# Earlier decode-state loads, an order for the down projection, and two wider spacings in a hybrid decoder step

## The chip, the cores and the metric

The kernel runs on one core of a Trainium2 chip. A core has TensorE (PE, matrix multiplication into the PSUM banks; its weight loads are listed apart as PEld), VectorE (DVE), ScalarE (ACT), GpSimd (POOL) and SyncE (SP), which here issues all DMAs from one queue. Each engine takes its instructions in a fixed order, and waits on semaphores for the others. The metric is the time of one execution in device microseconds; lower is better. The median of three runs is compared.

## What is computed

One inference step of a one-layer decoder, in float32, for a prompt of 1024 tokens and for 8 decode sequences of 4 tokens (32 tokens). D_MODEL is 1024, D_FF is 2816.

```python
def half_ffn(x, j, gpre, gpost):
    y = swiglu(rmsnorm(x, g[gpre]), ffn_w_gate[l, j], ffn_w_up[l, j], ffn_w_down[l, j])
    return x + 0.5 * rmsnorm(y, g[gpost])

x = half_ffn(x, 0, 0, 1)
h = rmsnorm(x, g[2])
(qm, km, vm, om, ip, fp), (qa, ka, va) = split_proj(h, w_in[l], b_gate[l])
u_m, new_m = mlstm_heads(qm, km, vm, om, ip, fp, mstate, mlstm_norm_gain[l], h.dtype)
...
x = x + rmsnorm(u @ w_out[l], g[3])
x = half_ffn(x, 1, 4, 5)
```

Here swiglu is `(silu(x @ w_gate) * (x @ w_up)) @ w_down`. The mLSTM has 4 heads, each with a 128 × 128 state matrix C and a normaliser n. The prompt starts from a zero state. Each of the 8 decode sequences brings its own C and n, from which its output is computed (`q @ C`) and which is then updated (decay × C + k v) and returned.

## The kernel before

**Tiles.** The 1056 tokens are four column blocks q = 0 to 3 of 264 columns (256 prompt tokens and 8 decode tokens). Two blocks form a half g. Activations lie transposed, features on the 128 partitions. Each float32 operand is split into a high part, which ScalarE casts (L200), and a low part, which VectorE subtracts (L201); a product is three matmuls: high × high, high × low, low × high. `K.od.now` is the planner's clock: a matmul of 264 columns adds 0.0025 + 264 / 2400 = 0.1125.

**Order.** `Order` is a planner in the kernel's own Python. The main line emits matmuls and advances the clock; side tasks (generators, `od.spawn`) are stepped when the clock reaches their due time, and a `yield w` sets the next due time w planner microseconds later. This gives the order of the program's text. The library then puts each engine's instructions in order when the program is built: the place in the text is the priority, but an instruction that is held back (by an operand, or by a buffer that isn't free) may be passed by later ones that are ready. After that the order in each engine's queue is fixed. `tc.issue_after(x)` keeps the instructions of its block behind x in the queue of x's engine, without a semaphore.

**Buffers.** A pool `slot` has 64 tiles of 128 × 528 floats (NSLOT). The sums of x, h, the reloaded h, the projections and the decode states all come from it. Weights come in through 3 `raw` tiles (L225). PSUM has banks `mm` (3), `a` (2), `b` (2) and `c` (1).

**Gate and up.** `ffn` runs 11 pairs p of hidden blocks; all but the first use a Strassen-like scheme of seven products (`PROD`) for each of gate (`mat` 0) and up (`mat` 1). Each product is 12 matmuls for each half g. Several of them add up in the `mm` and `b` banks in several steps, so partial sums must be copied out before the next product adds to the same bank: `nc.scalar.copy(sc[n][:, g], ps)` (L961) after the first, third and fifth product, and VectorE sums (L972, L978, L980) with them. The results h go to DRAM (`store_h`, L1027), except those of the last pair.

**Down.** `load_h` is a side task that brings h back for two blocks q at a time: per step m (of 22) two DMAs of 132 KB into slots `hq` (L1042) and a split on ScalarE and VectorE, then `yield HW` with HW = 0.6. It is first spawned at the beginning of the last pair's up half (L938); slots come free as the sums of x are used for the last time. Matmuls `pd` need h for each m. A later `load_h` (L995) prepares the next two blocks during the down projection.

**Decode.** `mlstm_sample` is the side task of the decode sequences. `state(b)` takes a slot, issues the DMA of C (L1635, 256 KB) and lets GpSimd put n beside it (L1636). Four states are loaded at its beginning, then two more at the beginning of each later pair of sequences, ahead of which the previous pair's updated states have been stored (L1696). In between it computes decayed scores `E`, masked keys (`kr`, its transposes `tT`, `kw`) and masked queries `qm`. Each pair then runs `sinter` (queries × C, output of 32 partitions), `sU` (keys × values, 32 rows) and the VectorE update L1691. The matmuls run between those of the output gates `po`, and later of the output projection `pw`.

**End.** For the last block q = 3, class `Last` brings output and residual back to token-major form. `residual` loads x, and after 14 planner microseconds does six groups of four transposes `xT` into a `b` bank, each copied out by ScalarE (L673), with `yield 2.0` after each group. `first`, `second` and `store_y` of block 2 use `b` banks as well (`yT`).

Of the kernel before, what the change touches and what calls it, by code (L numbers as in the profile page):

```python
# [1 line left out]

# [1 line left out]

# [27 lines left out]

XW = [2.0, 0.15, 0.2, 4.0, 3.0, 0.5]
PW = [4.0, 5.0, 1.0, 6.0, 4.5]
HW = 0.6

NHELD, NS = 5, 2
PQ = {1: [4.0, 8.0, 0, 8.0], 2: [2.0, 8.0, 0, 6.0], 3: [3.0, 7.0, 3.0, 0]}
# [113 lines left out]
def pe(K, out, lhsT, rhs, start=True, stop=True, tr=False, **kw):  # L152
    n = int(np.prod(rhs.shape[1:]))
    if tr:
        K.nc.tensor.transpose(out, lhsT, rhs)  # L155
        K.od.now += 0.11
        return
    K.nc.tensor.matmul(out, lhsT, rhs, start=start, stop=stop, **kw)  # L158
    if rhs.dtype == F32R:
        K.od.now += 0.0025 + (n if n >= 213 else 256) / 2400  # L160
    else:
        K.od.now += (4 if rhs.dtype == F32 else 1) * max(n, 64) / 2400


def nm(K, s):
# [479 lines left out]
class Last:  # L645
# [16 lines left out]
    def residual(self):  # L662
        K = self.K
        t = [slot(K, "x") for _ in range(4)]
        for kp in range(4):
            K.nc.sync.dma_start(t[kp], K.xs[self.q][kp])
        yield 14.0
        for x in range(2):
            for j in range(3):
                ps = bank(K, "xT", "b")  # L670
                self.turn(t, x, j, ps)
                self.x[j][x] = slot(K, "xT")[:, 0:512]
                K.nc.scalar.copy(self.x[j][x], ps)  # L673
                yield 2.0

    def block(self, mo, ps):
        K, nc = self.K, self.K.nc
# [216 lines left out]
def ffn(K, phase, j, gpost, nxt, gpre=None):  # L894
    nc, od = K.nc, K.od
    hs = {}
    for p in range(MT // 2):
        sg = {}
        if p == 0 and phase == 1:
            first_pair(K, sg)  # L900
            for (m, g), t in sg.items():
                hs[m, g] = store_h(K, m, g, t)
            continue
        if p < NPLAIN:

            ws = {}
            for q in range(NQ):
                g, s = q // 2, slice((q % 2) * QW, (q % 2) * QW + QW)
                for mat in range(2):
                    for m in range(2):  # L910
                        if q == 0:
                            ws[mat, m] = [od.take() for _ in range(2)]
                        if (m, g) not in sg:
                            sg[m, g] = slot(K, "h")
                        ps = bank(K, "pl", "ab"[mat])[:, 0:QW]
                        for k in range(KT):
                            od.need(("b", phase - 1, q, k // 2))
                            xh, xl = [x[:, k % 2] for x in K.X[q][k // 2]]
                            wh, wl = [w[:, k % 4] for w in ws[mat, m][k // 4]]
                            pe(K, ps, wh, xh, start=(k == 0), stop=False)  # L920
                            pe(K, ps, wh, xl, start=False, stop=False)
                            pe(K, ps, wl, xh, start=False, stop=(k == 7))
                            od.tick()
                        if p == 0 and (q, mat, m) in SUMS[phase]:
                            od.spawn(sums(K, phase - 1, SUMS[phase][q, mat, m]))
                        d = sg[m, g][:, s]
                        if mat == 0:
                            nc.scalar.activation(d, ps, AF.Silu)
                        else:
                            nc.vector.tensor_tensor(d, d, ps, op=ALU.mult)  # L930
            for (m, g), t in sg.items():
                hs[2 * p + m, g] = store_h(K, 2 * p + m, g, t)
            continue
        if phase == 1 and p == 4:
            mix_setup(K)
        for mat in range(2):
            if mat and p == MT // 2 - 1:
                od.spawn(load_h(K, hs, (0, 1)))  # L938
            bk, sc = {}, [None] * 3
            for i, (xi, tag, new) in enumerate(PROD):  # L940
                wh, wl = od.take()
                for g in range(NG):
                    if new:
                        bk[tag, g] = bank(K, "gu", tag)[:, 0:QW]
                    ps = bk[tag, g]
                    od.need(("S", phase - 1, g))
                    for k in range(4):
                        if xi > 2:
                            od.need(("s", phase - 1, g, xi, k // 2))
                        xh, xl = K.S[g][xi][k // 2]  # L950
                        xh, xl = xh[:, k % 2], xl[:, k % 2]
                        kw = {} if new else dict(skip_group_check=True)
                        pe(K, ps, wh[:, k], xh, start=(new and k == 0), stop=False, **kw)
                        pe(K, ps, wh[:, k], xl, start=False, stop=False, **kw)
                        pe(K, ps, wl[:, k], xh, start=False, stop=(k == 3), **kw)
                        od.tick()
                    if i in (0, 2, 4):
                        n = i // 2
                        if sc[n] is None:
                            sc[n] = pair(tmp(K, "sc", 2 * QW))  # L960
                        nc.scalar.copy(sc[n][:, g], ps)  # L961
                    for m, t, at, tg, n in OUT:
                        if at != i:
                            continue
                        if mat == 0:
                            if (m, g) not in sg:
                                sg[m, g] = slot(K, "h")
                            d = sg[m, g][:, t * QW:(t + 1) * QW]
                            if n is None:
                                nc.scalar.activation(d, bk[tg, g], AF.Silu)  # L970
                            else:
                                nc.vector.tensor_tensor(d, bk[tg, g], sc[n][:, g], op=ALU.add)  # L972
                                nc.scalar.activation(d, d, AF.Silu)  # L973
                        else:
                            d = sg[m, g][:, t * QW:(t + 1) * QW]
                            src = bk[tg, g]
                            if n is not None:
                                nc.vector.tensor_tensor(sc[n][:, g], src, sc[n][:, g], op=ALU.add)  # L978
                                src = sc[n][:, g]
                            nc.vector.tensor_tensor(d, d, src, op=ALU.mult)  # L980
        for (m, g), t in sg.items():
            if p < MT // 2 - 1:
                hs[2 * p + m, g] = store_h(K, 2 * p + m, g, t)
            else:
                hs[2 * p + m, g] = t
    h = K.h
    npd = 0
    steps = STEPS[phase]
    for si, step in enumerate(steps):
# [2 lines left out]
        last = Last(K, step[0], gpost) if nxt is None and si + 1 == len(steps) else None  # L992
        for mo in range(KT):
            if mo == 5 and si + 1 < len(steps):
                od.spawn(load_h(K, hs, steps[si + 1]))  # L995
            ps = {}
            for q in step:
                ps[q] = bank(K, "pd", "mm" if len(step) == 1 else ("mm", "a", "mm", "b", "mm", "a", "b")[npd % 7])[:, 0:QW]
                npd += 1
            for a in range(0, MT, 8):  # L1000
                for x, (dh, dl) in enumerate(od.take()):
                    for q in step:
                        for kk in range(dh.shape[1]):
                            m = a + 4 * x + kk
                            od.need(("h", q, m))
                            hh, hl = h[q, m][:, 0], h[q, m][:, 1]
                            pe(K, ps[q], dh[:, kk], hh, start=(m == 0), stop=False)
                            pe(K, ps[q], dh[:, kk], hl, start=False, stop=False)
                            pe(K, ps[q], dl[:, kk], hh, start=False, stop=(m == MT - 1))
                            od.tick()  # L1010
            if last:
                last.block(mo, ps[step[0]])
                continue
            for q in step:
                out_block(K, mo, ps[q], y[q], acc[q], gpost, tmp2 if si == 1 and mo > 5 else slot, tmp2)
# [12 lines left out]
    return h  # L1028


def load_h(K, hs, qs):

    nc = K.nc
    for m in range(MT):
        while (m, qs[0] // 2) not in hs:
            yield 0.3
        for q in qs:
# [6 lines left out]
            split(K, src, t[:, 0], t[:, 1])  # L1044
            K.h[q, m] = t
            K.od.done.add(("h", q, m))
        yield HW


def store_y(K, q, y):  # L1050
# [576 lines left out]
def mlstm_sample(K):  # L1627
# [3 lines left out]
    states = []  # L1631
# [9 lines left out]
    ps = bank(K, "n0T", "c")  # L1641
    pe(K, ps[:, 0:32], nrow, K.ident[0:32, 0:32], tr=True)
    n0 = K.kp.tile([P, 8, 4], F32, tag="n0", name="n0", bufs=1)
    nc.vector.tensor_copy(n0.rearrange("p b h -> p (b h)"), ps[:, 0:32])
    for b in range(4):
        state(b)
    E = scores(K, c, [K.sz[:, 6 + h] for h in range(HM)], [K.sz[:, 10 + h] for h in range(HM)], K.H[2][0], 32, slot)

# [11 lines left out]
    for hp in range(2):  # L1660
        q = slot(K, "qm")[:, 0:512]
# [7 lines left out]
    for b0 in range(0, 8, 2):  # L1669

        bs = (b0, b0 + 1)
        for b in range(len(states), min(b0 + 4, 8)):
            state(b)
        C = [states[b] for b in bs]
        for b, Cb in zip(bs, C):
            for h in range(HM):
# [3 lines left out]
        for hp in range(2):  # L1680
            pu = [bank(K, "sU", "ba"[hp]) for b in bs]
            for x in range(2):
                h = 2 * hp + x
                for b, ps in zip(bs, pu):
                    r = slice(32 * (b % 4), 32 * (b % 4) + 32)
                    pe(K, ps[:, x * 129:(x + 1) * 129], kb[b // 4][r, h * P:(h + 1) * P], K.vs[r, h],
                       start=True, stop=True)
# [328 lines left out]
```

## Time and profile before

| | |
|---|---|
| median of 3 runs | 2008.13 us (2006.71 to 2009.45) |
| profiled execution, its own time | 2009.42 us |
| span of its instructions | 2007.5 us |
| mean granted TensorE clock | 0.995 |
| HBM | read 171.38 MB, written 42.49 MB |

By stages of the profiled execution (us from the span's start; TensorE's idle time is the length less its busy time):

| stretch | what runs | PE busy | DVE busy | ACT busy | clock |
|---|---|---|---|---|---|
| 0 to 487 | first norm, gate and up of FFN 1 | 472.09 | 295.34 | 212.34 | 1.00 |
| 487 to 749 | down of FFN 1 | 261.33 | 121.25 | 108.66 | 1.00 |
| 749 to 1086 | input projection, attention, prompt mLSTM | 334.25 | 198.29 | 138.15 | 1.00 |
| 1086 to 1151 | output gates, decode states, prompt mLSTM | 63.43 | 44.28 | 33.05 | 0.89 |
| 1151 to 1257 | output projection | 106.00 | 71.45 | 60.65 | 1.00 |
| 1257 to 1724 | gate and up of FFN 2 | 464.25 | 291.91 | 191.99 | 1.00 |
| 1724 to 2007 | down of FFN 2, output | 274.10 | 145.53 | 128.41 | 0.99 |

How to read the profile: the granted clock is the TensorE clock that the throttle let through, as a share of full speed. A row of the timeline has start, duration, engine, line, operation, output <- inputs, shapes and count, and in brackets the engine's idle time before it with what ended it. Matmuls overlap in a pipeline, so the duration of one (some 284 ns for 264 columns) is longer than the distance from one to the next (some 122 ns). "The chain" is the chain of work that ended last, followed back from the end of the program: its pieces add up to the span.

### The profile page before, as it was taken

To read this page: it belongs to the slowest core of one execution; us is meant where nothing else is said; L and a number is where in the kernel's file an instruction comes from. 1 tells how busy PE (TensorE), PEld (TensorE's weight loads), DVE (VectorE), ACT (ScalarE), POOL (GpSimd) and SP (SyncE) were. 2 spreads that over 40 slices of the span, in tenths; PEclk is the share of its full clock that TensorE was granted. 3 is DMA by queue.
4 is the path that set the end of the run, shared out by engine and by line. 5 is a ranking of instruction groups with operands and counts; after the bars stand their busy time and mean duration, and the time that the engine had idled before them with its cause. 6 is when DMAs were issued, how large, how long until landed. Compare 5 with 4: busy or idle time off the path is not lost.

```text
span 2007.5 us, 40282 instructions
## 1 busy us (share of the span) xinstructions
PE 1975.5 (98%) x16108; PEld 1934.2 (96%) x16108; DVE 1168.1 (58%) x2801; ACT 873.2 (43%) x2097; POOL 40.0 (2%) x191
## 2 busy tenths in 40 slices
PE   7999999999999999999999999999999999999998
PEld 7999999999999999987999899999999999999998
DVE  7755555557238436467456657885555555624774
ACT  6533333336336332356243555453333334534563
POOL 1000000000000002000001000000000000000000
PEclk9999999999999999999999899999999999999999
DMA  6222222226247352201314134322222223635683
GB/s 231 70 75 91 82 64 85 75 90 191 88 130 225 101 142 91 65 1 38 88 53 135 49 110 139 119 76 85 64 84 77 86 74 101 178 111 172 200 257 121
DMA packets 281724, 216.68 MB, mean 108 GB/s; under 512 B 21096, under 2 KB 254688, under 8 KB 281536
## 3 DMA queue, kind: packets, MB, share of 16 engines
q1 hardware_dynamic: 281536, 214.11, 35.5%
q8 instruction: 126, 2.06, 0.4%
q14 instruction: 62, 0.51, 0.1%
HBM read 171.38 MB, written 42.49 MB: 107 GB/s over the span
## 4 chain that ended last, share of the span: by engine, by line
PE 92%; DVE 3%; ACT 2%; DMA 2%; issue 0%; SPq 0%; DVEq 0%; ACTq 0%
PE gu L158 40%; PE pd L158 25%; PE pz L158 7%; PE pw L158 5%; PE pl L158 3%; PE pv L158 2%; PE po L158 2%; ACT sws L1330 1%; PE cs L158 1%; PE swo L158 1%; PE E L158 1%; PE yT L155 1%; PE sws L158 1%; DMA hq<-h 1%; PE S L158 0%
## 5 line engine op out<-in xcount | busy, mean ns | idle before, releaser
L158 PE MATMUL gu<-Xh,wh 128*128 128x264 f32 x2240 | 636.5, 284 | 4.0 <-ACT sc L961 3.1
L158 PE MATMUL gu<-Xl,wh 128*128 128x264 f32 x2240 | 636.9, 284 | 0.0
L158 PE MATMUL gu<-Xh,wl 128*128 128x264 f32 x2240 | 635.8, 284 | 0.0
L158 PE MATMUL pd<-hq,wh 128*128 128x264 f32 x2816 | 521.1, 286 | 0.0
L201 DVE TENSOR_TENSOR wl<-raw,wh 128x512 fp32r<-128x512 f32 x450 | 298.3, 669 | 286.7 <-ACT wh L200 281.5
L158 PEld LDWEIGHTS pd<-hq,wh 128*128 128x128 f32 x2816 | 437.1, 189 | 0.1
L158 PEld LDWEIGHTS gu<-Xh,wh 128*128 128x128 f32 x2240 | 421.6, 188 | 4.7 <-ACT sc L961 3.5
L200 ACT CAST wh<-raw 128x512 fp32r<-128x512 f32 x450 | 267.7, 603 | 357.5 <-PE pd L158 227.2
L158 PEld LDWEIGHTS gu<-Xh,wl 128*128 128x128 f32 x2240 | 421.6, 188 | 0.0
L158 PEld LDWEIGHTS gu<-Xl,wh 128*128 128x128 f32 x2240 | 421.1, 188 | 0.0
L158 PE MATMUL pd<-hq,wl 128*128 128x264 f32 x1408 | 400.4, 284 | 0.0
L158 PEld LDWEIGHTS pd<-hq,wl 128*128 128x128 f32 x1408 | 264.8, 188 | 0.0
L961 ACT COPY sc<-gu 128x264 f32<-128x264 f32 x240 | 90.9, 379 | 354.7 <-PE gu L158 352.4
L201 DVE TENSOR_TENSOR wl<-ws,wh 128x512 fp32r<-128x512 f32 x160 | 108.8, 690 | 86.3 <-ACT wh L200 83.2
L972 DVE TENSOR_TENSOR h<-gu,sc 128x264 f32<-128x264 f32 x120 | 51.8, 432 | 142.2 <-PE gu L158 86.3
L978 DVE TENSOR_TENSOR sc<-gu,sc 128x264 f32<-128x264 f32 x120 | 51.8, 432 | 99.4 <-PE gu L158 51.6
L158 PE MATMUL pz<-xh,wh 128*128 128x264 f32 x352 | 102.3, 291 | 0.0
L158 PE MATMUL pz<-xh,wl 128*128 128x264 f32 x352 | 101.1, 287 | 0.0
L158 PE MATMUL pz<-xl,wh 128*128 128x264 f32 x352 | 100.7, 286 | 0.0
L973 ACT ACTIVATE h<-h 128x264 f32<-128x264 f32 x120 | 51.0, 425 | 107.9 <-DVE h L972 107.9
L200 ACT CAST wh<-ws 128x512 fp32r<-128x512 f32 x160 | 95.8, 623 | 2.5 <-DVE ws L775 2.4
L158 PE MATMUL pw<-uh,wh 128*128 128x264 f32 x256 | 73.8, 288 | 0.0
(405 smaller groups left out, 2966.9 us busy)
## 6 DMA issues: line engine op xcount, KB each, us to landing
raw<-ffn_w_down SPq DMA_DIRECT2D x80, 512.0 KB
raw<-ffn_w_gate SPq DMA_DIRECT2D x42, 512.0 KB
raw<-ffn_w_up SPq DMA_DIRECT2D x42, 512.0 KB
h<-h SPq DMA_DIRECT2D x80, 264.0 KB
hq<-h SPq DMA_DIRECT2D x160, 132.0 KB
raw<-ffn_w_down SPq DMA_DIRECT2D x40, 384.0 KB
x<-xs SPq DMA_DIRECT2D x48, 264.0 KB
raw<-w_in SPq DMA_DIRECT2D x21, 512.0 KB
```

Source lines behind the costliest of these rows:

```text
L155: K.nc.tensor.transpose(out, lhsT, rhs)
L158: K.nc.tensor.matmul(out, lhsT, rhs, start=start, stop=stop, **kw)
L200: K.nc.scalar.copy(hi, src)
L201: (eng or K.nc.vector).tensor_tensor(lo, src, hi.bitcast(F32), op=ALU.subtract)
L961: nc.scalar.copy(sc[n][:, g], ps)
L972: nc.vector.tensor_tensor(d, bk[tg, g], sc[n][:, g], op=ALU.add)
L973: nc.scalar.activation(d, d, AF.Silu)
L978: nc.vector.tensor_tensor(sc[n][:, g], src, sc[n][:, g], op=ALU.add)
L1330: nc.scalar.activation(s, s, AF.Exp, bias=nmx[:, y:y + 1], accum_out=den[:, y:y + 1])
```

## The change

Four edits. All eight decode states are loaded where four were, and the loads inside the loop go. Every first `pd` matmul (m = 0) is kept behind the last matmul of gate and up in TensorE's queue. The first `load_h` of each FFN is paced at 1.1 planner microseconds per step instead of 0.6; the later one keeps 0.6. The residual transposes of the last block are paced at 3.0 instead of 2.0.

```diff
-HW = 0.6
+HW = [1.1, 0.6]
...
-    K.nc.tensor.matmul(out, lhsT, rhs, start=start, stop=stop, **kw)
+    ins = K.nc.tensor.matmul(out, lhsT, rhs, start=start, stop=stop, **kw)
...
+    return ins.ins
...
                 K.nc.scalar.copy(self.x[j][x], ps)
-                yield 2.0
+                yield 3.0
...
-                od.spawn(load_h(K, hs, (0, 1)))
+                od.spawn(load_h(K, hs, (0, 1), HW[0]))
...
-                        pe(K, ps, wl[:, k], xh, start=False, stop=(k == 3), **kw)
+                        K.gu = pe(K, ps, wl[:, k], xh, start=False, stop=(k == 3), **kw)
...
-                od.spawn(load_h(K, hs, steps[si + 1]))
+                od.spawn(load_h(K, hs, steps[si + 1], HW[1]))
...
-                            pe(K, ps[q], dh[:, kk], hh, start=(m == 0), stop=False)
+
+                            with K.tc.issue_after(K.gu) if m == 0 else nullcontext():
+                                pe(K, ps[q], dh[:, kk], hh, start=(m == 0), stop=False)
...
-def load_h(K, hs, qs):
+def load_h(K, hs, qs, pace):
...
-        yield HW
+        yield pace
...
-    for b in range(4):
+    for b in range(8):
         state(b)
...
-        for b in range(len(states), min(b0 + 4, 8)):
-            state(b)
```

More of the change, by code (lines that the diff above doesn't have):

```diff
@@ L1 @@
-from contextlib import ExitStack
+from contextlib import ExitStack, nullcontext
 import numpy as np
```

## The prediction

> **What bounds the kernel now.** I read the page first, then TensorE's waits, then the order of time around each wait that the change touches. The page:
>
> ```profile
> span 2007.5 us, 40282 instructions
> PE 1975.5 (98%) x16108; PEld 1934.2 (96%) x16108; DVE 1168.1 (58%) x2801; ACT 873.2 (43%) x2097; POOL 40.0 (2%) x191
> PE 92%; DVE 3%; ACT 2%; DMA 2%; issue 0%; SPq 0%; DVEq 0%; ACTq 0%
> ```
>
> TensorE is busy for 98% of the span and is 92% of the chain that ended last. An edit that removes no matmul can win only where TensorE stands still or runs slowly. 2007.5 − 1975.5 = 32.0 us of standing still is all there is, and busy time may hide a low clock. The waits of TensorE (line, releaser: total, times, longest) name the places, and those of the change are:
>
> ```profile
> PE gu L158 <- ACT sc L961: 3.1, 2, 2.2
> PE sinter L158 <- DMA Cb<-state_mlstm_C: 1.2, 1, 1.2
> PE xT L155 <- ACT xT L673: 1.1, 1, 1.1
> PE gu L158 <- DVE sc L978: 0.9, 1, 0.9
> ```
>
> Together 6.3 us, 0.3% of the span. A measurement of this kernel can tell about 0.2%, or 4.0 us, from no change, so the waits alone would hardly show. The granted clock is the other place. In stretches of time (us, busy PE, PEld, DVE, ACT, POOL, clock, DMA share, GB/s):
>
> ```profile
> 1714.40:1716.60 2.20, 0.02 (x1) 0.02 (x1) 2.20 (x7) 2.20 (x8) 0.00 (x0) 1.00 0.90 269
> 1097.10:1100.50 3.40, 2.13 (x32) 1.41 (x30) 1.61 (x6) 0.30 (x1) 0.62 (x4) 1.00 1.01 290
> 1090.90:1094.30 3.40, 3.11 (x58) 2.47 (x58) 3.40 (x11) 0.24 (x1) 0.19 (x1) 1.00 0.34 61
> 1100.50:1114.10 13.60, 13.60 (x76) 11.06 (x70) 6.06 (x18) 3.83 (x4) 0.75 (x4) 0.50 0.54 159
> ```
>
> From 1100.5 to 1114.1 TensorE counts as fully busy, but at a clock of 0.50. This follows at once on the wait for a decode state, in the 3.4 us that hold 1.24 us of that wait and otherwise small matmuls.
>
> **Decode states.** Chain of waits, order of time on TensorE, DMA queue and POOL, around that place:
>
> ```profile
> 1087.69 2.28 PE po L158 x17
> ...
> 1091.19 0.72 PE sU L158 x8
> ...
> 1094.95 4.26 DMA Cb<-state_mlstm_C
> ...
> 1101.37 3.60 PE po L158 x15
> 1104.96 1.16 PE sU L158 x6
> ...
> 1109.18 4.26 PE po L158 x18
> 1113.44 1.70 PE E L158 x9
> ```
> ```profile
> 1093.95 0.94 SPq L1696 DMA_DIRECT2D o_s_C<-Cb  x2
> 1094.95 1.65 SPq L1635 DMA_DIRECT2D Cb<-state_mlstm_C  x2
> ```
> ```profile
> 1099.34 0.43 PE L158 MATMUL sinter<-Cb,qm 128*32 128x129 f32 x8 [1.24 <-DMA Cb<-state_mlstm_C]
> ```
>
> States 4 and 5 are asked for at 1094.95, behind the stores of states 0 and 1, and land 4.26 us later; `sinter` stands 1.24 us for them. With all eight loads at the start, states 4 and 5 leave right behind the first four, before 1091, over 8 us ahead of their use. The four loads moved forward are 4 × 256 KB = 1.05 MB; at the 290 GB/s of the stretch above that is 3.6 us, which fits. **Gain 1.24 us.**
>
> The slow stretch, priced by the same work at both clocks: 33 `po` matmuls took 3.60 + 4.26 = 7.86 us, and at 2.28 / 17 = 0.134 us would take 4.43 (3.43 lost). One pair of decode states took 1104.96 to 1109.18 = 4.22 us; two pairs had taken 1091.19 to 1094.95 = 3.76, so 1.88 each (2.34 lost). `E` took 1.70 against 1.31 in the row below (0.39 lost).
>
> ```profile
> 1118.92 1.31 PE E L158 x9
> ```
>
> Sum 6.2 us; ceiling 13.6 × 0.5 = 6.8. I take **6.2 us as gained**: the earlier stretch at 1090.9 held just as many small decode matmuls (58 in 3.4 us), with only 0.29 us idle, and kept 1.00. So it is the wait in such a stretch that I hold responsible. Bounds: 0 to 6.8.
>
> What the edit adds: four DMA issues on SP, at 1.65 / 2 = 0.83 us or less each, 3.3 us, ahead of the next `w_out` load; its first matmul in the chain comes at 1150.82, so they are hidden. On POOL, four more copies of the normaliser stand ahead of the key copy `kr`:
>
> ```profile
> 1087.21 0.95 POOL L1636 COPY Cb<-n 128x4 f32<-128x4 f32 x4
> 1088.10 0.61 POOL L1650 COPY kr<-sz 128x512 f32<-128x512 f32 x1
> ```
> ```profile
> 1089.81 0.60 PE L155 MATMUL tT<-ident,kr 128*128 128x128 f32 x4
> 1150.82 2.91 PE pw L158 x24
> ```
>
> That is 0.95 us of delay against 1089.81 − 1088.71 = 1.10 us between `kr` and the transposes that need it: cost 0, and up to 0.95 if the cover is gone. The 64 slots: by the code some 45 are live when the decode task starts (16 for the second half of x, 8 each of queries, keys and values left, attention, 5 gates), and it asks for 8 states and 6 more; that leaves about 5 for `uh`, `ul` and the last gates. It fits closely.
>
> **Ends of gate and up.** Both FFNs have the same picture. TensorE, ACT, DVE in order of time, then the `pd` matmuls executed before the last `gu` (same columns as the stretches):
>
> ```profile
> 478.48 0.39 PE L158 MATMUL gu<-Xh,wh 128*128 128x264 f32 x1 [0.90 <-ACT sc L961]
> 485.25 0.39 PE L158 MATMUL gu<-Xh,wh 128*128 128x264 f32 x1 [0.94 <-DVE sc L978]
> 1716.58 0.40 PE L158 MATMUL gu<-Xh,wh 128*128 128x264 f32 x1 [2.21 <-ACT sc L961]
> ```
> ```profile
> 1695.76 0.41 ACT L200 CAST hq<-hq 128x264 fp32r<-128x264 f32 x1
> ...
> 1715.22 1.03 ACT L200 CAST hq<-hq 128x264 fp32r<-128x264 f32 x3
> 1716.16 0.36 ACT L961 COPY sc<-gu 128x264 f32<-128x264 f32 x1
> ```
> ```profile
> 484.06 0.79 DVE L201 TENSOR_TENSOR hq<-hq 128x264 fp32r<-128x264 f32 x2 [1.14 <-ACT hq L200]
> 484.77 0.43 DVE L978 TENSOR_TENSOR sc<-gu,sc 128x264 f32<-128x264 f32 x1
> ```
> ```profile
> 477.00:486.78 9.78, 1.70 (x10) 1.52 (x11) 0.00 (x0) 1.00 0.98 281
> 1714.00:1723.72 9.72, 1.71 (x10) 1.51 (x11) 0.00 (x0) 1.00 0.91 264
> ```
>
> The fifth product's copy `sc` (L961) stands behind 27 casts of reloaded h (first and last of them shown); the sixth product adds to the same bank and waits for it. In the text, with a pace of 0.6, all 20 loads of h (40 casts) are called within 12 us; the copy's place is 4 × 24 + 12 matmuls at the planner's 0.1125 = 12.2 us. At a pace of 1.1 only m = 0 to 11, 24 casts, are called before it. So 3 casts fewer, at 1.03 / 3 = 0.34: the copy comes 1.0 us earlier. In FFN 1 that covers all of 0.90; in FFN 2 it leaves 1.2 of 2.21. The subtraction at 484.06 belongs to the last of 40 casts, and its priority falls behind L978, whose place is 13.5 us: 0.94 gone. **Gain 0.90 + 0.94 + 1.0 = 2.8 us**, at most 4.05.
>
> The loads themselves end at 20 × 1.1 = 22 us instead of 12, some 3 us into the down projection, which needs m = 19 only after 19 × 6 × 0.1125 = 12.8 us: covered.
>
> Keeping `pd` behind `gu` moves 10 matmuls in each FFN and removes none. They now fill waits, though: where the wait stays, TensorE stands bare for their time, 1.7 us at most. So below nothing this part can reach −3.4 us. I charge 0, because the waits they fill are those that the pace removes.
>
> **Residual transposes.** Six groups of four, from 1938.85 to 1951.50, 2.5 us apart, through two banks; the fourth waits for the second's copy:
>
> ```profile
> 1938.85 0.60 PE L155 MATMUL xT<-ident,x 128*128 128x128 f32 x4
> ...
> 1946.88 0.66 PE L155 MATMUL xT<-ident,x 128*128 128x128 f32 x4 [1.05 <-ACT xT L673]
> ...
> 1951.50 0.60 PE L155 MATMUL xT<-ident,x 128*128 128x128 f32 x4
> ```
> ```profile
> 1946.25 0.58 ACT L673 COPY xT<-xT 128x512 f32<-128x512 f32 x1
> ```
>
> At 3.0 instead of 2.0 the fourth comes about 3 us later, after 1949, when that copy is done at 1946.83. **Gain 1.05 us.** The last group moves to about 1957, and the next user of these banks is the output transposes at 1958.50: close, and worth up to 1 us if they meet.
>
> **Sum.** 1.24 + 6.2 + 2.8 + 1.05 = 11.3 us. The profiled execution took 2009.42 us (span 2007.5), 1.29 above the median 2008.13; the terms are the same for both, so I subtract from the median: 1996.8, and say **1997.0 us**.
>
> **Rivals.** *The clock stays.* Small decode matmuls, not the wait, lower it: they go on from 1091.19 with little between, and all four pairs remain. For it: the 2.21 us wait before 1716.58, longer but among full matmuls, kept 1.00. Against it: the stretch at 1090.9. Then only 1.24 + 2.8 + 1.05 = 5.1 us come: 2003.0. [...]
>
> *Nothing to see.* The casts stay where they are, since what is ready goes first whatever its place in the text, and lack of slots delays the new loads: the waits move and 2 us are left, 2006.
>
> *Slower.* The order put on `pd` takes away TensorE's filling while the waits stay. In FFN 2 the 2.21 us wait and 1.7 us of filling join into a bare gap near 3.9 us. It decides from a length between 2.21, which kept the clock, and 3.9 in one piece: then I count a spell like that at 1100.5. Two FFNs: 2 × (1.7 + 6.2) = 15.8 lost, 8.5 won at decode and end: 2015.4. Against it: the casts that make the waits are just those whose turn moves back.
>
> **Chances.** Forecast 0.47 (own range 1994 to 2000.5), clock stays 0.25, nothing 0.18, slower 0.10. The range runs from 1994.5 to 2009.0: it leaves out the slower case, a third of the third one and the edge of the first, 0.19. Faster by over 4.0 us (below 2004.1) are the forecast and two thirds of the second case, 0.63; within 0.2%: 0.26; slower 0.11.
>
> **What would show it.** Right: no `sinter` row with a DMA wait and a clock of 1.00 after it; all eight state loads together on the DMA queue; no `pd` before the last `gu`, and fewer than 27 casts ahead of the fifth copies; no wait at `xT`. Wrong: 0.50 again near the decode pairs; `gu` waits of the same length with nothing between; a new wait of the key transposes for POOL; `xT` or `yT` waiting at the end.

## The result and the profile after

| | time, us | profiled execution (span, mean clock) |
|---|---|---|
| before | 2006.81 median of 7 (2001.09 to 2009.45) | 2009.42 (2007.5, 0.995) |
| after | 1997.02 median of 7 (1994.33 to 1997.72) | 1995.35 (1993.5, 0.998) |

The ratio is 0.9950, with a 95% interval of 0.9938 to 0.9962: faster by 0.5%. The prediction said 1997.0 in a range of 1994.5 to 2009.0.

The page of after (span; busy time by engine; the chain's shares):

```profile
span 1993.5 us, 40262 instructions
PE 1967.7 (99%) x16108; PEld 1928.7 (97%) x16108; DVE 1166.4 (59%) x2801; ACT 871.6 (44%) x2097; POOL 39.6 (2%) x191
PE 92%; DVE 3%; DMA 3%; ACT 2%; issue 0%; SPq 0%; DVEq 0%; ACTq 0%
```

TensorE executes the same 16108 matmuls, yet it is busy for 7.8 us less: busy time held slow matmuls, as the 0.50 clock had shown. It stands still for 1993.5 − 1967.7 = 25.8 us, where it was 32.0. What is left of the waits that the change touches, after (line, releaser: total, times, longest):

```profile
PE gu L158 <- ACT sc L962: 1.8, 2, 1.1
PE sU L158 <- DVE kw L1533: 0.8, 1, 0.8
PE pd L158 <- DVE wl L202: 0.2, 1, 0.2
```

The waits for a decode state (1.2) and for the residual's copy (1.1) are gone; those at `gu` fell from 4.05 to 1.81; `sU` waits 0.78 where it waited 0.29. (Line numbers of after are 1 to 3 higher.)

The decode stretch carries most of the result. These rows of single tiles (duration, first to last start) mark its ends, first of before, then of after:

```profile
L155 PE MATMUL n0T<-ident,n x1: 247/247/247, 1086.7 to 1086.7; 32*128 32x32 f32 x1
L155 PE MATMUL snT<-ident,nn x1: 273/273/273, 1116.1 to 1116.1; 128*32 128x128 f32 x1
L155 PE MATMUL shT<-ident,snum x1: 273/273/273, 1129.6 to 1129.6; 128*128 128x128 f32 x1
```
```profile
L155 PE MATMUL n0T<-ident,n x1: 247/247/247, 1083.8 to 1083.8; 32*128 32x32 f32 x1
L155 PE MATMUL snT<-ident,nn x1: 273/273/273, 1104.9 to 1104.9; 128*32 128x128 f32 x1
L155 PE MATMUL shT<-ident,snum x1: 273/273/273, 1118.5 to 1118.5; 128*128 128x128 f32 x1
```

From `n0T` to `shT` it was 42.9 us and is 34.7, **8.2 us less**; from `n0T` to `snT` 29.4 and 21.1. The clock in this stretch of after (us, busy PE, PEld, DVE, ACT, POOL, clock, DMA share, GB/s):

```profile
1088.30:1091.70 3.40, 2.88 (x54) 2.24 (x56) 3.40 (x10) 0.00 (x0) 0.09 (x1) 1.00 1.18 280
1091.70:1100.50 8.80, 8.80 (x110) 7.75 (x107) 8.41 (x27) 3.03 (x4) 1.46 (x6) 1.00 0.73 198
1100.50:1104.90 4.40, 4.40 (x36) 3.97 (x34) 1.91 (x7) 2.33 (x6) 0.38 (x2) 1.00 0.80 236
```

It stays at 1.00. But 1.24 us of wait and about 6 us of clock, less the 0.49 by which `sU` waits longer, make 6.7 and not 8.2. The rest is seen by setting the small matmuls of before (first fence, the pairs from state 4 on) against those of after:

```profile
1097.16 0.93 PE L158 MATMUL sU<-vs,kw 32*128 32x129 f32 x10
1099.34 0.43 PE L158 MATMUL sinter<-Cb,qm 128*32 128x129 f32 x8 [1.24 <-DMA Cb<-state_mlstm_C]
1099.70 0.49 PE L158 MATMUL sU<-vs,kw 32*128 32x129 f32 x4
1100.21 0.43 PE L158 MATMUL sinter<-Cb,qm 128*32 128x129 f32 x8
```
```profile
1094.79 0.65 PE L158 MATMUL sinter<-Cb,qm 128*32 128x129 f32 x16
1095.37 1.17 PE L158 MATMUL sU<-vs,kw 32*128 32x129 f32 x16
1098.49 0.65 PE L158 MATMUL sinter<-Cb,qm 128*32 128x129 f32 x16
1099.07 1.16 PE L158 MATMUL sU<-vs,kw 32*128 32x129 f32 x16
```

The text of the pair loop puts all `sinter` ahead of `sU`, and after executes its last two pairs so. In the kernel before, the library had put each state's `sinter` between groups of `sU` there; that it expected the states late is the likely reason, but is not shown. The prediction took the order of these matmuls for given.

At the end of gate and up, ScalarE in after:

```profile
474.60 1.14 ACT L201 CAST wh<-raw 128x512 fp32r<-128x512 f32 x2 [1.38 <-DMA raw<-ffn_w_down]
475.65 0.41 ACT L201 CAST hq<-hq 128x264 fp32r<-128x264 f32 x1
475.96 0.37 ACT L962 COPY sc<-gu 128x264 f32<-128x264 f32 x1
```

The copy that `gu` waits for is still late. 21 casts of h stand ahead of it where there were 27, but now ScalarE's queue is held 1.38 us by the cast of a weight that has not landed.

After has a spell of half clock as well, in the prompt's attention, where neither kernel was expected to have one. It is not the change's: six of the 13 profiles have it, among them that of the spacing alone, where the states are late.

```profile
965.80:967.80 2.00, 2.00 (x16) 1.73 (x15) 0.91 (x6) 0.00 (x0) 0.00 (x0) 0.95 0.76 216
967.80:971.20 3.40, 3.40 (x16) 3.21 (x17) 1.99 (x18) 0.06 (x1) 0.19 (x1) 0.53 0.31 86
```

It follows on transposes and matmuls of 32 rows or columns with TensorE busy all the time, and costs 3.4 × 0.47 = 1.6 us. The two profiles differ by 14.1 us. Of that 8.2 are the decode stretch, 2.2 the `gu` waits, 1.05 the residual, 1.0 the first wait of the program (7.11 and 6.07, which the change does not touch) and 0.7 a wait at `kcT` that comes and goes between executions; the spell takes 1.6 back. That is 11.6 of 14.1. Another 1.1 lies at the start: the `pl` matmuls there follow one another at 0.22 us until 18.5 us in before, and at 0.12 from 15.3 us on in after, so that from the first `xsT` to the first `gu` before takes 63.75 us and after 62.61 (the views give a clock of 1.00 for both all the same). 1.4 us are not attributed.

### The profile page after: what moved, and what is told of

It reads as the page before. It is cut to its first block, busy times and chain, and to the rows that moved or that the text cites. A ratio compares the mean times of both kernels' runs of the same rounds, so it can differ in the third digit from the quotient of the medians.

```text
span 1993.5 us, 40262 instructions
## 1 busy us (share of the span) xinstructions
PE 1967.7 (99%) x16108; PEld 1928.7 (97%) x16108; DVE 1166.4 (59%) x2801; ACT 871.6 (44%) x2097; POOL 39.6 (2%) x191
## 4 chain that ended last, share of the span: by engine, by line
PE 92%; DVE 3%; DMA 3%; ACT 2%; issue 0%; SPq 0%; DVEq 0%; ACTq 0%
PE gu L158 40%; PE pd L158 24%; PE pz L158 7%; PE pw L158 5%; PE pl L158 3%; PE pv L158 2%; PE po L158 2%; DMA raw<-ffn_w_down 1%; ACT sws L1333 1%; PE cs L158 1%; PE swo L158 1%; PE E L158 1%; PE yT L155 1%; PE sws L158 1%; DMA hq<-h 0%; PE S L158 0%
```

## The experiments

All times are medians with their range; the ratio is to the kernel before, executed beside it on the same chip. There were eleven runs in three sessions, one of them the changed kernel again.

**The states alone, and the whole change again.** The kernel before with only this edit:

```diff
-    for b in range(4):
+    for b in range(8):
         state(b)
...
-        for b in range(len(states), min(b0 + 4, 8)):
-            state(b)
```

> The kernel before with all eight decode states loaded at the start of the decode task; the other three edits are left out. My theory: the 1.24 us wait of sinter goes and with it the half clock near it (6.2 us), so 5.5 to 7.5 us less than before, near 2000 us, and a profile without 0.50 between 1085 and 1115. The rival, that the small decode matmuls lower the clock by themselves: 0.8 to 1.3 us less, and 0.50 again somewhere in that stretch. In both: a wait of sU on kw of 0.5 to 0.9 us, because four more copies stand ahead of kr on POOL.

Measured: 1996.97 (1995.45 to 2003.13), ratio 0.9967 (0.9957 to 0.9978). Its stretch from `n0T` to `shT` is 34.6 us at a clock of 1.00. The whole change:

> The changed kernel as it is, on the same chip as the three runs beside it. The theory that the eight states alone carry the gain: it lies at the time of the run with the states alone, 1996 to 1998, within 1 us of it. The rival, that the spacing, the order and the residual transposes add the 2.8 + 1.05 us of the prediction: 1993 to 1995. Mean granted clock .998 or more in nearly every execution.

Measured: 1996.53 (1994.37 to 1997.14), ratio 0.9957 (0.9941 to 0.9972). By means, the states alone lie 1.6 us above it, with an interval of 0.0 to 3.2 across the two sessions: the three other edits bring something between nothing and 3 us. **The states carry the gain.**

**Spacing of the reloads, and the order of the down projection.** Three kernels from before, and after without the order:

```diff
-HW = 0.6
+HW = [1.1, 0.6]
```

> The kernel before with only the pace of the first reload of h at 1.1 instead of 0.6. If the pace is what shortens the waits at the ends of gate and up, they fall from 1.84 and 2.21 us to about 1.2 and 0.7 as in the changed kernel, and the time is 2 to 2.5 us less than before. If it is the order of pd that counts, the waits stay near 4 us in sum and pd matmuls still run ahead of the last gu; then the time is as before.

```diff
+                            with K.tc.issue_after(K.gu) if m == 0 else nullcontext():
+                                pe(K, ps[q], dh[:, kk], hh, start=(m == 0), stop=False)
```

> The kernel before with only the order edit: every first pd matmul behind the last gu. My theory: the waits of gu for sc keep their causes, the casts of h at a pace of 0.6, and TensorE now stands bare where pd filled in: gu waits of 5 to 7.5 us in sum instead of 4.05, time up by 1 to 3.4 us. The rival, that the pd matmuls running ahead were themselves what made the waits: waits under 3 us, time 1 to 2 us less than before.

Both edits together:

> The kernel before with the pace of 1.1 and with pd kept behind gate and up; states and residual as before. My theory: as the pace alone, 2 to 2.5 us less than before, with gu waits of 1.2 and 0.7 us; the order adds nothing, since few pd matmuls find a gap. The rival: the order takes away filling, so the time is 1 us above that of the pace alone.

The changed kernel with the order taken out again:

> The changed kernel without the order of the down projection behind gate and up (states, spacing and residual transposes stay). The theory that the order leaves TensorE standing where the down projection had filled in: 0.5 to 2 us faster than the changed kernel, with matmuls of pd ahead of the last ones of gu and the waits of gu at 1.9 or less. The rival, that the order is needed so that the last gate and up product is not put back: 0.5 to 2 us slower.

| kernel | time, us | ratio | `gu` waits, us |
|---|---|---|---|
| spacing alone | 2002.01 (1997.04 to 2006.73) | 0.9988 (0.9974 to 1.0002) | 1.9 |
| order alone | 2005.68 (2002.26 to 2011.39) | 1.0006 (0.9992 to 1.0020) | 5.6 |
| spacing and order | 2003.66 (1998.13 to 2006.62) | 0.9994 (0.9982 to 1.0006) | 2.0 |
| after without order | 1995.78 (1993.26 to 1996.85) | 0.9952 (0.9934 to 0.9970) | 1.6 |

The spacing alone leaves waits of 0.8 and 1.1 us, in sum as expected, but a time that cannot be told from that of before. The order alone does what the prediction's slower case described, on a smaller scale. Its waits in FFN 1, and the clock around the second:

```profile
477.15 0.39 PE L158 MATMUL gu<-Xh,wh 128*128 128x264 f32 x1 [0.98 <-ACT sc L962]
483.90 0.39 PE L158 MATMUL gu<-Xh,wh 128*128 128x264 f32 x1 [1.88 <-DVE sc L979]
```
```profile
482.00:483.90 1.90, 0.02 (x1) 0.00 (x1) 1.19 (x4) 1.62 (x5) 0.00 (x0) 1.00 1.05 306
484.90:488.30 3.40, 3.40 (x18) 3.40 (x17) 3.40 (x8) 2.10 (x5) 0.00 (x0) 0.52 0.49 136
```

0.94 us of wait became 1.88, bare, and a spell of 3.4 us at 0.52 followed. With the spacing the order has nothing to hold: after without it also executes no `pd` ahead of the last `gu`, its waits are 1.6 (the two profiles of after show 1.8 and 1.6), and its time is 0.75 us below that of after by means (interval −2.4 to 0.9). That `pd` would fill the waits, as expected of this run, was wrong.

The size of the spacing's gain depends on the execution it is set against. Without the spacing, the profiles of before, of the residual edit and of the states alone show 4.05, 2.9 and 2.2 us of `gu` waits; with it, nine profiles of this record, two of them of after, show 1.3 to 2.1. The states-alone kernel still has 27 casts ahead of the copy.

**Residual transposes alone.**

```diff
-                yield 2.0
+                yield 3.0
```

> The kernel before with the residual's transposes spread by 3.0 in place of 2.0 and nothing else. By the prediction's step: the wait of 1.05 us ahead of the transposes goes, 0 to 1 us faster, which the timing can hardly tell (ratio .9993 to 1.000). The rival: the later transposes hold the first matmuls that need x, 0.5 to 1 us slower, with a new wait behind the xT copy.

Measured: 2002.42 (1998.76 to 2008.08), ratio 0.9990 (0.9977 to 1.0003). The wait of 1.05 us is not among its waits, and no new one at `xT` or `yT` is. Agrees, but the time cannot tell it from nothing. This profile is of more use for the decode states: they are late in it, with a wait of 1.67 us, and yet its clock stays at 1.00. `n0T` to `snT`:

```profile
L155 PE MATMUL n0T<-ident,n x1: 247/247/247, 1085.3 to 1085.3; 32*128 32x32 f32 x1
L155 PE MATMUL snT<-ident,nn x1: 273/273/273, 1109.1 to 1109.1; 128*32 128x128 f32 x1
```

23.8 us, against 21.1 with the early states: 2.7 to 2.8 us more without any loss of clock. Waits explain (1.67 + 0.29) − 0.78 = 1.2 of it. The other 1.6 are the order: in this kernel's row of small matmuls, the pair at 1102.02,

```profile
1102.02 0.71 PE L158 MATMUL sU<-vs,kw 32*128 32x129 f32 x6
1102.66 0.43 PE L158 MATMUL sinter<-Cb,qm 128*32 128x129 f32 x8
1103.01 0.49 PE L158 MATMUL sU<-vs,kw 32*128 32x129 f32 x4
1103.43 0.43 PE L158 MATMUL sinter<-Cb,qm 128*32 128x129 f32 x8
1103.79 0.71 PE L158 MATMUL sU<-vs,kw 32*128 32x129 f32 x6
1104.43 0.39 PE L158 MATMUL po<-xh,wh 128*128 128x264 f32 x1
```

takes 1104.43 − 1102.02 = 2.41 us. The same pair grouped, in the second execution of after, runs from 1094.31 to 1095.98:

```profile
1094.31 0.65 PE L158 MATMUL sinter<-Cb,qm 128*32 128x129 f32 x16
1094.88 1.16 PE L158 MATMUL sU<-vs,kw 32*128 32x129 f32 x16
1095.98 0.39 PE L158 MATMUL po<-xh,wh 128*128 128x264 f32 x1
```

1.67 us: 0.74 less. The pair before it, 1095.76 to 1099.99 with the wait of 1.67 in it, is 0.89 above 1.67. Together 1.63 us, for six more changes between kinds of matmul.

**Wait and order taken apart.** Before and after differ in both, so two kernels hold one of them each. After, with the last two pairs' matmuls put by hand in the alternating order (the update is moved behind both halves of `sU`):

```diff
+        late = b0 >= 4
...
+                    if late and n in (3, 5):
+                        i = (3, 5).index(n)
+                        with K.tc.issue_after(last):
+                            mark = inter(bs[i], C[i])
```

> The changed kernel with all eight states early, but the matmuls of its last two batches put by hand in the order that they have in the kernel before: three of sU, the four of sinter for one state, three of sU, the four of sinter for the other, two of sU. Theory: this order by itself costs 1.6 us, because each change between sinter and sU costs; the transpose n0T to the transpose snT takes 22.4 to 22.9 us in place of 21.1, and the time is 1.5 us above the changed kernel's. Rival: the order is free and what was seen hidden is another wait on the DMA: 21.1 us. On the clock: if the wait on the DMA is what lowers it, no execution is at .995 or less; if it is the thin order, some are.

After, with the states late again but the order held by hand:

```diff
-    for b in range(8):
+    for b in range(4):
...
+        for b in range(len(states), min(b0 + 4, 8)):
+            state(b)
...
+                    with K.tc.issue_after(last):
+                        pe(K, ps[:, x * 129:(x + 1) * 129], kb[b // 4][r, h * P:(h + 1) * P], K.vs[r, h],
```

> The changed kernel with the states loaded late again, four ahead and two more at each batch, as in the kernel before, but with the matmuls of each batch held in the changed kernel's order (all of sinter, then all of sU). Theory: the wait on the DMA is back, 1.2 to 2.0 us, but not the 1.6 us of the order: n0T to snT takes 22.3 to 23.3 us in executions at full clock, and in a quarter to half of the executions the mean clock is .995 or less, so 3 to 5 us slower than the changed kernel on the mean. Rival, that the alternating order and not the wait lowers the clock: no execution at .995 or less, and 1 to 2 us slower than the changed kernel.

And after with no spacing between the pairs, so that small matmuls follow on one another:

```diff
-BW = 2.4
+BW = 0.0
```

> The changed kernel with the spacing of the decode batches set from 2.4 to 0, so that small matmuls stand against one another with no dense ones between. The theory that a wait is needed to lower the clock: granted clock 1.00 between 1085 and 1105, mean clock .998, and the time moves only by waits on VectorE and on the banks, 0 to 3 us. The rival, that a stretch of small matmuls lowers it without a wait: windows at .50 in or just behind 1088 to 1105 in the profile, mean clock .997 or less over the executions, 3 to 6 us slower.

| kernel | time, us | ratio | `n0T` to `snT` |
|---|---|---|---|
| early, alternating | 2000.80 (1998.37 to 2002.93) | 0.9988 (0.9977 to 0.9998) | 24.5 |
| late, grouped | 2002.86 (1998.99 to 2004.09) | 1.0001 (0.9992 to 1.0011) | 24.2 |
| early, no spacing | 2004.12 (2000.29 to 2010.07) | 0.9995 (0.9981 to 1.0008) | 25.4 |

(Set these beside each other rather than by ratio: the kernel before had 2005.92 in the session of the last and 2002.01 in that of the first two, where fewer of its executions lost clock.)

The alternating order costs more than expected: 24.5 − 21.1 = 3.4 us, with no wait beyond the 0.78 of `sU` and a clock of 1.00 through it. Of this 0.7 is not the order's, for 75 `po` matmuls lie in its stretch where after has 69, and six at 0.122 us take that long; 2.7 us are left. (From `n0T` to the last `pw`, where both kernels execute the same 1386 matmuls, it is 165.1 − 161.9 = 3.2.) Its pairs are cut twice more, by `po` in their middle: eight changes between kinds for each pair where after has three. Ten more changes for 2.7 us are 0.27 each, and six for 1.63 were 0.27. **Some 0.3 us for each change**, under which TensorE counts as busy. The whole kernel is 4.6 us slower than after by means, where 1.5 was expected; what lies beyond the 3.2 is open. The traces show one thing that goes with a change. In before the first weight load of `sinter` starts at 1091.84, 0.20 us after the last `sU` matmul has started, with its own matmul only 0.002 us behind it, while among these `sU` a load starts 0.11 us ahead of its matmul (1091.30 and 1091.41). In after a load of `po` starts 0.12 us ahead of its matmul (1094.33 and 1094.45), but from `po` to `sinter` the load starts 0.21 us after the last `po` matmul (1094.79 and 1094.58). Why it waits is not shown.

The late and grouped kernel did not get the wait that was meant: `sinter` moved behind `po` and no longer waits for the DMA. In its place `sU` waits for the VectorE update of a pair before:

```profile
1090.46 0.65 PE L158 MATMUL sinter<-Cb,qm 128*32 128x129 f32 x16
1092.12 1.23 PE L158 MATMUL sU<-vs,kw 32*128 32x129 f32 x8 [1.01 <-DVE Cb L1695]
```
```profile
1091.10:1092.10 1.00, 0.00 (x1) 0.00 (x0) 1.00 (x4) 0.00 (x0) 0.00 (x0) 1.00 0.80 178
1092.10:1095.20 3.10, 3.08 (x19) 2.55 (x19) 3.07 (x12) 0.00 (x0) 0.38 (x2) 0.99 0.34 99
1095.20:1098.60 3.40, 3.40 (x22) 2.92 (x24) 1.31 (x4) 0.62 (x1) 0.63 (x4) 0.50 0.83 231
```

Here 1.01 us of wait among small matmuls, ended by VectorE and not by a DMA, stands ahead of 3.4 us at 0.50. (One of this kernel's eleven executions has a mean clock of .995 or less, where a quarter to a half were expected.) Without spacing the clock halves with no wait near it: from 1089.20 on TensorE counts as busy throughout, on small matmuls alone for 7.2 us, and then

```profile
1089.20:1096.40 7.20, 7.17 (x113) 5.57 (x113) 7.20 (x24) 0.00 (x0) 1.17 (x4) 1.00 1.06 267
1096.40:1100.60 4.20, 4.20 (x26) 3.28 (x24) 3.28 (x11) 0.00 (x0) 0.98 (x3) 0.96 0.55 164
1100.60:1117.20 16.60, 16.60 (x74) 14.07 (x74) 5.86 (x19) 4.27 (x14) 0.19 (x1) 0.50 0.23 66
```

16.6 us at 0.50. So no wait was needed here; thin work was enough. (VectorE is busy for all of the 7.2 us, so there TensorE may be paced by it within what counts as busy. From `n0T` to `snT` this kernel executes 43 `po` matmuls, not 69, so its 25.4 us in the table cannot be set beside the others.)

**Where the wait falls.** The traces show a difference between executions in which the clock halved and those in which it did not. In before and in after every change of the clock lies a whole number of steps of 3.413 us behind its first rise: in before the rise is at 18.52 us, where the `pl` matmuls go from 0.22 us to 0.12, and the drop at 1100.55, 317 steps on; in after they are at 15.27 and 967.59, 279 steps apart. In late and grouped, by the clock of its stretches, the drops at 968.9 and 1095.15 lie 37 steps apart. The spells that end before the program does last 1 step in after, 2 with spacing and order, 4 in before and with the spacing alone, and 5 without spacing. The first rise differs between executions, so the steps cut the same work elsewhere. These are the step ahead of the drop in before, and the two steps around the wait of the residual edit:

```profile
1097.13:1100.55 3.42, 2.15 (x31) 1.41 (x30) 1.58 (x6) 0.27 (x1) 0.62 (x4) 1.00 1.00 289
```
```profile
1094.42:1097.84 3.42, 2.27 (x22) 1.94 (x20) 2.27 (x9) 0.62 (x1) 0.63 (x4) 1.00 0.67 186
1097.84:1101.25 3.41, 2.88 (x32) 2.23 (x33) 2.22 (x8) 0.00 (x0) 0.19 (x1) 1.00 1.03 291
```

In before one step holds the whole wait, and no `po` matmul starts in it. With the spacing alone (a wait of 2.00 us) and with spacing and order (1.31) one step holds the whole wait too, with no and five `po`, and the clock halves behind it, for 13.65 and 6.83 us. In the residual edit the two steps above part at 1097.84, within the wait of 1.67 us (1096.69 to 1098.36; no change of its clock is near to mark the boundary), ten `po` start in each, and the clock stays at 1.00; so it is with the order alone (1.89 us, parted at 1099.13, 180 steps behind its drop at 484.7; nine `po` in each). In these five profiles the clock goes with the place of the wait, not with its length. Without spacing the 7.2 us themselves keep 1.00; the drop comes behind the step from 1096.84 to 1100.25, which has five `po` among `sU`. In late and grouped, 0.4 us of the wait fall into the step ahead of the drop, 1091.74 to 1095.15, which has three `po`. How thin a step must be is not settled: states alone kept 1.00 behind 3.16 us, 1089.75 to 1092.91, in which no `po` starts but 28 `sinter` do.

The mean clock of every execution shows how often a kernel pays:

```
                                     executions at a mean clock of .995 or less
late, alternating: before                     34 of 83
late, alternating: with one or two edits      15 of 48
late, grouped                                  1 of 11   (five more at .996)
early, alternating                             0 of 12
early, no spacing                              3 of 12   (two more at .996)
early, grouped: states alone, after, no order  0 of 36
```

Of the kernel before, those 34 took 2007.1 us on average and the 34 at .998 or more 2001.4: **the long spell costs 5.7 us and comes in two executions of five.** After's 14 executions average 1996.4. (The mean clock does not say where the half clock lay; that it lay among the decode states in all 34 is inferred from the profiles. Nor are short spells counted: 6.8 us of half clock among the states, with spacing and order, gave a mean of .997.)

**The copies on GpSimd.** After without the order, with the eight copies of the normaliser written behind `kr`:

> The changed kernel without the order of the down projection, and with the eight GpSimd copies Cb<-n behind the copy kr. Theory: the wait of sU on kw (0.78 us) falls to 0 to 0.3, n0T to snT takes 20.4 to 20.8 us in place of 21.1, and the time is 0.5 us below that of the kernel without the order (1995.8), too little to tell by the timing. Rival: the copies now come late for sinter, which waits on GpSimd by 0.3 to 1 us: same or slower by as much.

Measured: 1995.91 (1994.26 to 1996.11), ratio 0.9962 (0.9948 to 0.9976); `sU` waits 0.78 as in after. The edit did not take hold: the library still put the copies first, as its GpSimd rows show.

```profile
1084.02 1.44 POOL L1655 COPY Cb<-n 128x4 f32<-128x4 f32 x8
1085.39 0.61 POOL L1652 COPY kr<-sz 128x512 f32<-128x512 f32 x1
```
```profile
1087.10 0.60 PE L155 MATMUL tT<-ident,kr 128*128 128x128 f32 x4
1088.49 0.71 PE L158 MATMUL sU<-vs,kw 32*128 32x129 f32 x8 [0.78 <-DVE kw L1533]
```

It answers the question all the same. `kr` is done at 1086.00 and the transposes start at 1087.10, so GpSimd does not hold them. They come later in TensorE's queue than before, behind all of the `po` matmuls instead of ahead of the last four, and `sU` lost that cover: 0.78 − 0.29 = 0.49 us. This kernel and the one without the order are the lowest measured, and neither alone can be told from after. Both lack the order; their ten executions together lie 1.0 us below after's 14 by means (interval 0.05 to 1.95, across sessions), so the order may cost something.

## Why the prediction was right, and where it was not

**Decode states: the step right, its sum short by 0.8 us in the profile, and a term missing.** 1.24 + 6.2 = 7.4 was predicted for an execution with the spell, 8.2 came. Clock: 5.7 between executions with and without the spell, for 6.2 predicted. The 0.5 too much was the order's: the pair that took 4.22 us was set against 1.88, which pairs in another order had taken, but the same pair takes 2.41 at full clock in the residual edit, so that 1.81 of its 2.34 us were the clock. Wait: 1.24 less the new 0.49 at `sU`, 0.75. Not foreseen: 1.6 us, since the library puts `sinter` and `sU` of the last two pairs in another order when the states are loaded early. The three make 8.05. "Cost 0" on GpSimd held, but the transposes lost cover on another queue, TensorE's own.

**The clock's cause: half right.** The prediction held "the wait in such a stretch" responsible, and gave a quarter to the rival that small matmuls alone do it. The runs show both: a wait of 1.24 to 2.0 us that falls whole into one step of 3.413 us among small matmuls (before, spacing alone, spacing and order), or a thin step with little or no wait (0.4 us in late and grouped, none without spacing). Cut by a boundary, waits of 1.67 and 1.89 us left the clock at 1.00. So the prediction's profile had the spell by luck of the execution, and none of the 36 with the states early and grouped has a mean clock as low. The rival did not come true for this change: in after full matmuls stand between the pairs, 9, 12 and 13 `po` in the steps from 1090.47 to 1100.71; that they are what keeps the clock is argued from the run without spacing.

**Ends of gate and up: mis-sized.** 2.8 us were predicted from one profile with 4.05 us of waits. The 0.94 us behind VectorE went as said. But that execution was an unfavourable one (others without the spacing show 2.2 and 2.9), and what is left, 1.8 and 1.6 in the two profiles of after, has another cause: "24 casts ahead" became 21, but the copy now stands behind a weight cast that waits for its DMA. By the mean of three profiles without it and nine with it, some 1.3 us.

**The order of `pd`: charged 0, and no gain** once the spacing is there (if anything, a loss of 1.0 us). Without the spacing it is 1.6 us slower than before by means (interval −0.5 to 3.7), with bare waits and half clock in its profile: the slower rival in small. No run shows a bare gap near 3.9 us at the end of gate and up, from which that rival counted a spell; with the order alone 2.04 us ahead of 1710.80 kept 1.00, and 1.88 us ahead of 483.90 were followed by 0.52.

**Residual: 1.05 us of wait gone**, as said, below what the timing tells.

**The sum.** An execution of before with the spell takes 2007.1, after 1996.4: 10.7 us, of which decode explains 8.05 and the rest is some 2.7, where 11.3 = 7.4 + 3.85 was predicted. The base helped: 2008.13, the median of three, stood for executions with the spell. Over all 83 executions before averages 2004.2, and the gain 7.8. That the forecast met the median to 0.02 us is luck: decode came 0.6 larger than its terms, the rest 1.2 smaller, and the base was 1.3 above the median of seven.

## What to carry to other kernels

Look for a low clock inside "busy" time, and then at how many executions have it, before pricing it from one profile. Here each further change of kind among small matmuls cost some 0.27 us; with no full ones between the pairs the clock was at half for 16.6 us; and waits of 1.24, 1.31 and 2.00 us among them were followed by 13.65, 6.83 and 13.65 us of it. So it is worth trying to group small matmuls by kind, to break them up by full ones, and to let nothing wait among them. A load moved early can change the order that a scheduler gives to the matmuls behind it, so compare that order too.

## What the runs showed of the hardware that was not expected

A further change between the kinds `sinter`, `sU` and `po` cost about 0.3 us (0.27 in the residual edit and in early and alternating), counted as busy. The first weight load of `sinter` started 0.20 us after the last `sU` matmul in before, and 0.21 us after the last `po` matmul in after, where among `po` a load starts 0.12 us ahead of its matmul. In before and after the clock changed only at whole steps of 3.413 us behind its first rise, which came at 18.52 and 15.27 us. A wait that one step held whole was followed by half clock in three profiles (1.24, 1.31 and 2.00 us), and one that was cut between two steps was not in two (1.67 and 1.89). The clock halved with TensorE busy throughout as well (965.8 to 967.8 in after, transposes and matmuls of 32 rows or columns, then 0.53), and it stayed low for one step or for several: 3.41 us in after, 13.65 in before, 17.07 without spacing.
